# A hybrid attention block on one core: row combinations, key rotary work and value splits moved within the first stage, a store moved behind a load, other PSUM banks

## The chip, the cores and the metric

The kernel runs on one core of one Trainium2 chip. The metric is the device time of one execution in microseconds (us); lower is better. A measurement is the median of several runs. Beside it one execution was recorded by the hardware profiler, and every row of a profile here comes from such an execution.

## The reference, cut to what matters

The block normalises x (512 tokens, 2048 features), projects it with one large matrix, and runs two groups of attention heads on the result. The first group takes keys and values three ways: compressed over blocks of 32 tokens, selected in blocks, and over a window. The stage that the change touches makes the keys and values, with the two small networks that compress them:

```
h = rmsnorm(x, norm_g);  proj = h @ w_in
kc = compress(rope(k_cmp), cmp_k_pos, cmp_k_w1, cmp_k_w2)
vc = compress(v_cmp,       cmp_v_pos, cmp_v_w1, cmp_v_w2)
   # compress: 31 overlapping blocks of 32 tokens, flat @ w1 (4096 x 256), silu, @ w2 (256 x 128)
k_sel, k_win = rope(...);  v_sel, v_win = ...
```

The rest (attention, gates, output projection with residual, final norm) follows in later stages that the diff leaves alone.

## The kernel before, in words

All matrix products are made from pairs of words. A float is split into a high word (a copy rounded to the narrower form that TensorE multiplies) and a low word (what is left). `load_unit` (line 85) does this for weights: a DMA brings a raw tile, ScalarE writes the high word `whi` (line 95), VectorE subtracts it from the raw tile into the low word `wlo` (line 96). `mm3` (line 121) then makes three matmuls, lines 122 to 124. The words stand in three rotating buffers, the raw tiles of the compression weights in two.

The first stage has these parts. Two passes over `w0` make the compressed keys and values (`acc0`) and the selected and window keys (`acc1`). In the second of them, while TensorE works, `blocks_part` (line 219) builds the shifted blocks F0 and F1 for the compression. Then come two loops of eight units. Each unit of the first loop is a token chunk (`tok_chunk`, line 258: 24 matmuls of 256 columns with weights `w1s`, the selected values) and a compression unit (`compress_unit`, line 230: eight matmuls, lines 236 and 237, into `kacc`). The second loop does the same with `w2s` (24 matmuls of 408 columns) and F1 into `vacc`. Between them `compress_hidden` (line 245) and lines 382 to 390 finish the compressed keys: copy the sums, two small matmuls with E2 (line 250), tanh, two small matmuls with `cw2s` (line 383).

Beside these loops other work is dealt out to units by hand:

- `build` (line 284) makes, from two row groups of x, the sums and differences that later products need (lines 303 to 307), and their high and low words (lines 309 and 310). For the first four groups these go to one buffer, `ft`, 1 MB in all, which `write` (line 313) stores to DRAM (line 316) before it loads the next rows (line 281). The buffer is single, so the next group's words wait for the store.
- `k_evac` (line 348) turns one key accumulator with the rotary tables: three products (lines 127 to 129), a sum (line 350), high and low word (lines 354 and 355).
- `v_evac` (line 371) scales a value accumulator into float (line 373) and splits it (line 375 on ScalarE, line 376 on GpSimd).

The order of instructions on each engine is made by a scheduler, which runs the program in a model of time as it is written down. `issue_after` ties the instructions of a block behind a given one on the same engine; the variables `last["hi"]`, `last["lo"]` and `last["dma"]` hold the latest high word, low word and load. All loads and stores here go through SyncE's queue (SP), one after the other; one that waits holds up those behind it.

PSUM has eight banks. In the first loop the token sums stand in banks 0 and 1, `kacc` in 2, keys in 4 to 7. `hp` and `kcp` of the compressed keys take bank 3, and the second loop's four token sums take banks 4, 5, 2, 3 in this order, `vacc` bank 0.

Of the kernel before, what the change touches and what calls it, by code (L numbers as in the profile page):

```python
# [10 lines left out]
F32 = mybir.dt.float32  # L11
F32R = mybir.dt.float32r
AF = mybir.ActivationFunctionType
ALU = mybir.AluOpType
# [3 lines left out]
P = 128  # L18
S = 512
D = 2048  # L20
KT = D // P
NQ = S // P
# [13 lines left out]
def hybrid_block(ctx, tc, xT, xtm, w0, w1s, w2s, wz, wq, wkb, wo0, wos, cw1, cw2, cpos, rope, tabs, sinks, gT, fg, out):  # L36
# [28 lines left out]
    fd = dram("fd", 4, 2, P, KT // 4, 256)  # L65
# [5 lines left out]
    last = {}  # L71
# [67 lines left out]
    def tmp(name):  # L139
        return s0b.tile([P, S], F32, name=name, tag="tmp", bufs=5)  # L140
# [103 lines left out]

    def compress_hidden(b, acc):
        a1 = s0b.tile([P, 256], F32, name="a1", tag="a1", bufs=1)
        act.activation(a1, acc[:, 0:256], AF.Copy)
        hp = bank(3 if b == 0 else 0)
        for i in range(2):
            pe.matmul(hp[:, i * 64:i * 64 + 64], a1[:, i * P:(i + 1) * P], E2, start=True, stop=True)  # L250
        th = s0b.tile([P, P], F32, name="th0", tag="th0", bufs=1)
        act.activation(th, hp[:, 0:P], AF.Tanh, scale=0.5)
        sl = s0b.tile([P, 2, 64], F32, name="sl", tag="sl", bufs=1)
        dve.scalar_tensor_tensor(out=sl.rearrange("p a b -> p (a b)"), in0=th, scalar=1.0, in1=hp[:, 0:P],
                                 op0=ALU.add, op1=ALU.mult)
        return sl

    def tok_chunk(wsrc, width, accs, shared, u):
        hi, lo = load_unit(wsrc[:, u], 2 * width, place=MOVING)
        for j in range(2):  # L260
            k = 2 * u + j
            for t in range(NQ):
                ts = slice(t * P, (t + 1) * P)
                first = k == 0 and not (shared and t % 2)
                mm3(accs[t], xh[:, k, ts], xl[:, k, ts], hi[:, j * width:(j + 1) * width],
                    lo[:, j * width:(j + 1) * width], first, k == KT - 1 and (t % 2 == 1 or not shared))
# [14 lines left out]
        nc.sync.dma_start(xr, xT[:, 2 * m:2 * m + 2, :])  # L281
        todo.append((m, xr))

    def build():
        m, xr = todo.pop(0)
        if m < 4:
            ft = kvp.tile([P, 8, 256], F32, name="ft", tag="VL")
            words = [[ft[:, 2 * f + e, :].bitcast(F32R) for e in range(2)] for f in range(4)]
            out = [(fd.rearrange("f e p m c -> p (f e) m c")[:, :, m, :], ft)]
        else:  # L290
            if m % 2:
                two = tmp("fq"), s0.tile([P, NQ, P], F32, name="fv", tag="vbs").rearrange("p a b -> p (a b)")
            else:
                two = (s0b.tile([P, S], F32, name="sq", tag="sq", bufs=1),
                       s0.tile([P, S], F32, name="sqa", tag="sqa"))
            two = [t.rearrange("p (e c) -> p e c", e=2) for t in two]
            words = [[pu[2 * (2 * f + e) + 1][:, m - 4, :] for e in range(2)] for f in range(2)]
            words += [[t[:, e, :].bitcast(F32R) for e in range(2)] for t in two]
            out = [(fw[f].rearrange("e p m c -> p e m c")[:, :, m - 4, :], t) for f, t in enumerate(two)]
        ge, go = [gt[:, 2 * m + e:2 * m + e + 1] for e in range(2)]  # L300
        a11, a21, a12, a22 = xr[:, 0, H0], xr[:, 0, H1], xr[:, 1, H0], xr[:, 1, H1]
        with tc.issue_after(last["lo"]), tc.issue_after(last["hi"]):
            act.activation(xr[:, 1, :], xr[:, 1, :], AF.Copy, scale=go)
            dve.tensor_tensor(out=a21, in0=a11, in1=a21, op=ALU.subtract)
            dve.scalar_tensor_tensor(out=a11, in0=a11, scalar=ge, in1=a12, op0=ALU.mult, op1=ALU.subtract)
            dve.scalar_tensor_tensor(out=a12, in0=a21, scalar=ge, in1=a12, op0=ALU.mult, op1=ALU.subtract)
            dve.tensor_tensor(out=a22, in0=a22, in1=a12, op=ALU.add)
            for (hi, lo), src, scale in zip(words, (a11, a12, a21, a22), (1.0, -1.0, ge, 1.0)):
                act.activation(hi, src, AF.Copy, scale=scale)
# [3 lines left out]
        def write():  # L313
            with tc.issue_after(last["dma"]):
                for dst, src in out:
                    nc.sync.dma_start(dst, src)
# [9 lines left out]
    for u in range(KT // 2):  # L326
        hi, lo = load_unit(w0[1, :, u], 1024)
        with tc.issue_after(last["lo"]):
            for job in work[u]:
                job()  # L330
        if u < 2:
            with tc.issue_after(last["dma"]):
                rows(u)
        if u == 6:
            with tc.issue_after(last["dma"]):
                for e in range(2):
                    nc.sync.dma_start(xd[e], even[e])
# [33 lines left out]
    def v_evac(t, w, ps):  # L371
        vt = VF[:, t // 2, w, :] if t % 2 else tmp("vt")[:, 0:256]
        act.activation(vt, ps[:, 0:256], AF.Copy, scale=rstd[:, t:t + 1])
        vg = vt.rearrange("p (g c) -> p g c", g=2)
        act.activation(VH[:, :, t, w, :], vg, AF.Copy)
        pool.tensor_tensor(out=VL[:, :, t, w, :], in0=vg, in1=VH[:, :, t, w, :].bitcast(F32), op=ALU.subtract)

    for j in (1, 3, 5, 7):
        pu[j] = yp.tile([P, 4, 256], F32R, name=f"pu{j}", tag=f"yp{j}")
    sl = compress_hidden(0, kacc)  # L380
    kcp = bank(3)
    for i in range(2):
        pe.matmul(kcp[:, 0:64], cw2s[:, 0, i, :], sl[:, i, :], start=i == 0, stop=i == 1)
    kct = s0.tile([P, 64], F32, name="kct")
# [38 lines left out]
    def words_out():  # L423
        vbs = s0.tile([P, NQ, P], F32, name="vbs", tag="vbs")
        for t in range(NQ):
            v_evac(t, 1, sacc2[t])
# [592 lines left out]
    def write(t, n, q=None):  # L1019
        (q or nc.sync).dma_start(out[:, t, n * 512:n * 512 + 512], xs[n][t // 2][:, t % 2, :])  # L1020
# [359 lines left out]
```

## Time and profile before

| what | value |
|---|---|
| median of 3 runs | 819.78 us (819.44 to 820.15) |
| the profiled execution | 820.54 us |
| its span from the first to the last instruction | 818.8 us |
| TensorE clock granted | 0.998 |
| busy share: TensorE, VectorE, ScalarE | 98%, 81%, 59% |
| HBM | 110.31 MB read, 17.07 MB written |

How to read the profile: a row of the timeline gives the start and the length in us, the engine (PE is TensorE, PEld its weight loads, DVE is VectorE, ACT is ScalarE, POOL is GpSimd, SP the queue of SyncE), the line of the kernel, the operation, output and inputs by name, shape and count; in square brackets stands how long the engine was idle before it and what ended that. Rows of the same line that follow each other are merged. A row of the windows gives the busy time of each engine in a stretch, the clock that was granted, the busy share of the DMA engines, and GB/s. The chain that ended last follows the work back from the last instruction. Matmuls overlap, and their ends are modelled; their starts are what can be relied on.

### The profile page before, as it was taken

How to read it: one execution, taken by the hardware profiler on the slowest of the kernel's cores; microseconds unless marked ns; L12 is line 12 of the kernel's file. 1: busy time of each engine (PE TensorE's matmuls, PEld its weight loads, DVE VectorE, ACT ScalarE, POOL GpSimd, SP SyncE). 2: the span in 40 equal slices, each digit the busy share in tenths (PEclk: the TensorE clock that was granted, in tenths of full speed). 3: DMA queues.
4: the chain of work that ended last, by engine and by line, in shares of the span. 5: the costliest groups of instructions: out<-in, count | busy, mean ns of one | idle time of the engine just before them, and what ended most of it. 6: DMA issues, size and time to landing. Idle time of an engine off the chain costs nothing.

```text
span 818.8 us, 14134 instructions
## 1 busy us (share of the span) xinstructions
PE 805.6 (98%) x5281; PEld 733.7 (90%) x5281; DVE 666.6 (81%) x1326; ACT 483.6 (59%) x1026; POOL 67.7 (8%) x54
## 2 busy tenths in 40 slices
PE   9999999999999999999999999999999999999996
PEld 8888898999999999999988888888888888999996
DVE  7859786966889899899876688887687799777895
ACT  6734456564867687786756365645444657543545
POOL 4500002020000000000011211011001000000000
PEclk9999999999999999999999999999999999999999
DMA  9665786898421322423742422222222257497845
GB/s 327 201 204 168 264 289 226 258 333 306 137 85 33 116 78 93 168 83 99 233 141 68 138 78 55 75 87 69 78 78 77 77 145 260 145 244 205 242 99 205
DMA packets 52116, 128.30 MB, mean 157 GB/s; under 512 B 4944, under 2 KB 17232, under 8 KB 52048
## 3 DMA queue, kind: packets, MB, share of 16 engines
q1 hardware_dynamic: 50032, 120.59, 43.9%
q0 software_dynamic: 1728, 6.29, 4.4%
q8 instruction: 41, 0.67, 0.3%
q10 hardware_dynamic: 288, 0.52, 0.2%
q14 instruction: 27, 0.22, 0.1%
HBM read 110.31 MB, written 17.07 MB: 156 GB/s over the span
## 4 chain that ended last, share of the span: by engine, by line
PE 85%; DVE 5%; DMA 4%; ACT 3%; issue 2%; POOL 1%; SPq 0%; DVEq 0%; ACTq 0%; POOLq 0%
PE pj L124 16%; PE pj L123 16%; PE pj L122 16%; PE bank L124 4%; PE bank L122 4%; PE oa L123 4%; PE bank L123 4%; PE oa L122 4%; PE oa L124 3%; PE sp L557 3%; DMA rw<-wos 2%; PE tp L595 2%; PE tp L879 2%; DMA xr<-xT 1%; PE spb L844 1%
## 5 line engine op out<-in xcount | busy, mean ns | idle before, releaser
L124 PE MATMUL pj<-xh,wlo 128*128 128x512 f32 (+1 forms) x560 | 194.9, 348 | 1.8 <-DVE wlo L635 1.8
L122 PE MATMUL pj<-xh,whi 128*128 128x512 f32 (+1 forms) x560 | 194.7, 348 | 0.0
L123 PE MATMUL pj<-xl,whi 128*128 128x512 f32 (+1 forms) x560 | 194.6, 347 | 0.0
L96 DVE TENSOR_TENSOR wlo<-raw,whi 128x1024 fp32r<-128x1024 f32 (+2 forms) x102 | 116.7, 1148 | 34.8 <-ACT whi L95 29.4
L95 ACT ACTIVATE whi<-raw 128x1024 fp32r<-128x1024 f32 (+1 forms) x101 | 95.0, 943 | 76.9 <-PE pj L123 22.8
L124 PEld LDWEIGHTS pj<-xh,wlo 128*128 128x128 f32 x560 | 105.4, 188 | 15.0 <-DVE wlo L635 2.4
L123 PEld LDWEIGHTS pj<-xl,whi 128*128 128x128 f32 x560 | 105.3, 188 | 13.1 <-issue 0.9
L122 PEld LDWEIGHTS pj<-xh,whi 128*128 128x128 f32 x560 | 105.3, 188 | 12.2
L635 DVE TENSOR_TENSOR wlo<-raw,whi 128x1024 fp32r<-128x1024 f32 x49 | 59.5, 1220 | 9.3 <-ACT whi L634 9.2
L634 ACT ACTIVATE whi<-raw 128x1024 fp32r<-128x1024 f32 x49 | 51.1, 1054 | 21.1 <-DVE raw L684 6.1
L123 PE MATMUL oa<-wlo,yh 128*128 128x256 f32 (+1 forms) x168 | 50.2, 299 | 0.1
L122 PE MATMUL oa<-whi,yh 128*128 128x256 f32 (+1 forms) x168 | 49.8, 298 | 0.6 <-ACT yh L954 0.6
L124 PE MATMUL oa<-whi,yl 128*128 128x256 f32 (+1 forms) x168 | 49.5, 298 | 0.0
L858 ACT ACTIVATE ttb<-ttb,sums 128x256 f32<-128x256 f32 (+1 forms) x64 | 30.1, 471 | 26.5 <-DVE sums L851 26.1
L525 ACT ACTIVATE ph<-tp 128x512 fp32r<-128x512 f32 x56 | 32.4, 592 | 14.9 <-PE tp L595 8.7
L123 PE MATMUL bank<-wlo,xh 128*128 128x256 f32 (+1 forms) x128 | 40.3, 317 | 0.3 <-DVE wlo L96 0.3
L124 PE MATMUL bank<-whi,xl 128*128 128x256 f32 (+1 forms) x128 | 39.9, 314 | 0.0
L526 DVE TENSOR_TENSOR pl<-tp,ph 128x512 fp32r<-128x512 f32 x56 | 37.8, 684 | 1.9 <-ACT ph L525 1.8
L122 PE MATMUL bank<-whi,xh 128*128 128x256 f32 (+1 forms) x128 | 36.7, 318 | 1.5 <-ACT whi L95 1.5
L122 PE MATMUL bank<-xh,whi 128*128 128x512 f32 x96 | 37.3, 400 | 0.0
L123 PE MATMUL bank<-xl,whi 128*128 128x512 f32 x96 | 36.9, 389 | 0.0
L573 ACT ACTIVATE tt<-tt,sums 128x128 f32<-128x128 f32 (+3 forms) x64 | 35.3, 554 | 1.2 <-DVE sums L563 1.2
(359 smaller groups left out, 2172.6 us busy)
## 6 DMA issues: line engine op xcount, KB each, us to landing
raw<-wz SPq DMA_DIRECT2D x36, 512.0 KB, 3.6
raw<-wq SPq DMA_DIRECT2D x28, 512.0 KB, 3.7
raw<-cw SPq DMA_DIRECT2D x16, 512.0 KB, 4.6
raw<-wos SPq DMA_DIRECT2D x12, 512.0 KB, 4.6
rw<-wos SPq DMA_DIRECT2D x10, 512.0 KB, 5.6
xr<-xT SPq DMA_DIRECT2D x16, 256.0 KB, 5.0
raw<-w SPq DMA_DIRECT2D x8, 512.0 KB, 4.5
fd<-ft SPq DMA_DIRECT2D x4, 1024.0 KB, 6.2
```

What stands on the lines that cost most here:

```text
L95: last["hi"] = act.activation(hi[:, :width], rw[:, :width], AF.Copy).ins
L96: last["lo"] = dve.tensor_tensor(out=lo[:, :width], in0=rw[:, :width], in1=hi[:, :width].bitcast(F32), op=ALU.subtract).ins
L122: pe.matmul(ps, ah, bh, start=first, stop=False, skip_group_check=go_on)
L123: pe.matmul(ps, ah, bl, start=False, stop=False, skip_group_check=go_on)
L124: recent["mm"] = pe.matmul(ps, al, bh, start=False, stop=last, skip_group_check=go_on).ins
L525: act.activation(ph, tp, AF.Copy)
L526: dve.tensor_tensor(out=pl, in0=tp, in1=ph.bitcast(F32), op=ALU.subtract)
L557: pe.matmul(sp[:, a:b], qq[:, qs], kk[0][:, ko:ko + b - a], start=pi == 0, stop=pi == 2)
L573: act.activation(tv, tv, AF.Exp, bias=mn[:, i, 1 + w:2 + w], scale=-1.0, accum_out=dn[:, i, 1 + w:2 + w])
L634: act.activation(hi, src, AF.Copy)
L635: last["lo"] = dve.tensor_tensor(out=lo, in0=src, in1=hi.bitcast(F32), op=ALU.subtract).ins
L858: act.activation(tv, tv, AF.Exp, bias=mn[:, e, v:v + 1], scale=-1.0, accum_out=dn[:, e, v:v + 1])
```

## The change

- The third `build` is cut in two: its arithmetic stays in unit 7 of the pass before, its splits into `ft` go behind the words of the first loop's token unit 1. The fourth `build` moves from unit 3 to unit 4, and its store from unit 6 to unit 7.
- `k_evac` moves from behind the compression units 1 and 5 to ahead of 2 and 6 in the first loop, and from behind 1 and 4 to ahead of 2 and 4 in the second.
- `v_evac` is cut in two. The scaled copies of the first values go directly behind the copy of `kacc`; their splits go behind the words of the second loop's token unit 1.
- `hp` and `kcp` go to bank 1 in place of 3, and the second loop's token sums to banks 4, 5, 3, 2.

```diff
     def compress_hidden(b, acc):
         a1 = s0b.tile([P, 256], F32, name="a1", tag="a1", bufs=1)
-        act.activation(a1, acc[:, 0:256], AF.Copy)
-        hp = bank(3 if b == 0 else 0)
+        last["a1"] = act.activation(a1, acc[:, 0:256], AF.Copy).ins
+        if b == 0:
+            with tc.issue_after(last["a1"]):
+                vts.extend(v_scaled(t, 0, sacc[t]) for t in range(NQ))
+        hp = bank(1 if b == 0 else 0)
...
-    def build():
+    def build(part=False):
         m, xr = todo.pop(0)
...
-            for (hi, lo), src, scale in zip(words, (a11, a12, a21, a22), (1.0, -1.0, ge, 1.0)):
-                act.activation(hi, src, AF.Copy, scale=scale)
-                dve.scalar_tensor_tensor(out=lo, in0=src, scalar=scale, in1=hi.bitcast(F32), op0=ALU.mult,
-                                         op1=ALU.subtract)
...
+        def split_rows():
+            words, out = places()
+            with tc.issue_after(last["lo"]), tc.issue_after(last["hi"]):
+                for (hi, lo), src, scale in zip(words, (a11, a12, a21, a22), (1.0, -1.0, ge, 1.0)):
+                    act.activation(hi, src, AF.Copy, scale=scale)
+                    dve.scalar_tensor_tensor(out=lo, in0=src, scalar=scale, in1=hi.bitcast(F32), op0=ALU.mult,
+                                             op1=ALU.subtract)
+            writes.append(lambda: write(out))
...
-        writes.append(write)
+        if part:
+            return split_rows
+        split_rows()
...
-        if u in (3, 5, 7):
+        if u in (3, 5):
             build()
+        if u == 7:
+            third = build(True)
...
     for u in range(8):
         tok_chunk(w1s, 256, sacc, True, u)
+        if u == 1:
+            third()
+        if u in (2, 6):
+            with tc.issue_after(last["lo"]):
+                k_evac(0, u // 6)
         compress_unit(F0, 0, u, kacc)
-        if u in (1, 5):
-            with tc.issue_after(last["lo"]):
-                k_evac(0, u // 5)
-        if u in (2, 6):
+        if u in (2, 7):
             writes.pop(0)()
-        if u == 3:
+        if u == 4:
             build()
...
     sl = compress_hidden(0, kacc)
-    kcp = bank(3)
+    kcp = bank(1)
...
-    for t in range(NQ):
-        v_evac(t, 0, sacc[t])
-    sacc2 = [bank(t) for t in (4, 5, 2, 3)]
+    sacc2 = [bank(t) for t in (4, 5, 3, 2)]
     vacc = bank(0)
     for u in range(8):
         tok_chunk(w2s, 408, [a[:, 0:408] for a in sacc2], False, u)
-        compress_unit(F1, 1, u, vacc)
-        if u in (1, 4):
+        if u == 1:
+            with tc.issue_after(last["hi"]):
+                for t in range(NQ):
+                    v_split(t, 0, vts[t])
+        if u in (2, 4):
             with tc.issue_after(last["lo"]):
                 k_evac(1, u // 4)
+        compress_unit(F1, 1, u, vacc)
```

`v_scaled` and `v_split` are the two halves of `v_evac`. The places into which a group is split (`places`) are now taken when the splits are written down.

More of the change, by code (lines that the diff above doesn't have):

```diff
@@ L282, in rows, with places @@
         todo.append((m, xr))
-    def build():
+    def build(part=False):
         m, xr = todo.pop(0)
[L286 to L292, printed above, removed]
-            else:
[L294 to L299, printed above, removed]
+        def places():
+            if m < 4:
+                ft = kvp.tile([P, 8, 256], F32, name="ft", tag="VL")
+                words = [[ft[:, 2 * f + e, :].bitcast(F32R) for e in range(2)] for f in range(4)]
+                out = [(fd.rearrange("f e p m c -> p (f e) m c")[:, :, m, :], ft)]
+            else:
+                if m % 2:
+                    two = tmp("fq"), s0.tile([P, NQ, P], F32, name="fv", tag="vbs").rearrange("p a b -> p (a b)")
+                else:
+                    two = (s0b.tile([P, S], F32, name="sq", tag="sq", bufs=1),
+                           s0.tile([P, S], F32, name="sqa", tag="sqa"))
+                two = [t.rearrange("p (e c) -> p e c", e=2) for t in two]
+                words = [[pu[2 * (2 * f + e) + 1][:, m - 4, :] for e in range(2)] for f in range(2)]
+                words += [[t[:, e, :].bitcast(F32R) for e in range(2)] for t in two]
+                out = [(fw[f].rearrange("e p m c -> p e m c")[:, :, m - 4, :], t) for f, t in enumerate(two)]
+            return words, out
         ge, go = [gt[:, 2 * m + e:2 * m + e + 1] for e in range(2)]
@@ L307, in build, with write @@
             dve.tensor_tensor(out=a22, in0=a22, in1=a12, op=ALU.add)
-            for (hi, lo), src, scale in zip(words, (a11, a12, a21, a22), (1.0, -1.0, ge, 1.0)):
-                act.activation(hi, src, AF.Copy, scale=scale)
-                dve.scalar_tensor_tensor(out=lo, in0=src, scalar=scale, in1=hi.bitcast(F32), op0=ALU.mult,
-                                         op1=ALU.subtract)
-        def write():
+        def split_rows():
[6 more added lines that the diff above has]
+            writes.append(lambda: write(out))
+        def write(out):
             with tc.issue_after(last["dma"]):
@@ L361, in hybrid_block, with v_scaled, v_split @@
         tok_chunk(w1s, 256, sacc, True, u)
+        if u == 1:
[3 more added lines that the diff above has]
+                k_evac(0, u // 6)
         compress_unit(F0, 0, u, kacc)
-        if u in (1, 5):
-            with tc.issue_after(last["lo"]):
-                k_evac(0, u // 5)
-        if u in (2, 6):
+        if u in (2, 7):
             writes.pop(0)()
-        if u == 3:
+        if u == 4:
             build()
-    def v_evac(t, w, ps):
+    def v_scaled(t, w, ps):
         vt = VF[:, t // 2, w, :] if t % 2 else tmp("vt")[:, 0:256]
         act.activation(vt, ps[:, 0:256], AF.Copy, scale=rstd[:, t:t + 1])
+        return vt
+    def v_split(t, w, vt):
         vg = vt.rearrange("p (g c) -> p g c", g=2)
@@ L379, in hybrid_block @@
         pu[j] = yp.tile([P, 4, 256], F32R, name=f"pu{j}", tag=f"yp{j}")
+    vts = []
     sl = compress_hidden(0, kacc)
-    kcp = bank(3)
+    kcp = bank(1)
     for i in range(2):
@@ L425, in words_out @@
         for t in range(NQ):
-            v_evac(t, 1, sacc2[t])
+            v_split(t, 1, v_scaled(t, 1, sacc2[t]))
             act.activation(vbs[:, t, :], sacc2[t][:, 256:384], AF.Copy, scale=rstd[:, t:t + 1])
```

## The prediction

> **What bounds the kernel now.** I read the page first, then the windows of the first stage, then the starts of single matmuls there, because the change touches nothing outside that stage.
>
> ```profile
> PE 805.6 (98%) x5281; PEld 733.7 (90%) x5281; DVE 666.6 (81%) x1326; ACT 483.6 (59%) x1026; POOL 67.7 (8%) x54
> PE 85%; DVE 5%; DMA 4%; ACT 3%; issue 2%; POOL 1%; SPq 0%; DVEq 0%; ACTq 0%; POOLq 0%
> ```
>
> TensorE (PE) is busy for 98% of the span and makes up 85% of the chain that ended last. No matmul is added or removed, so the only thing to win is time in which PE stands still. Ends of matmuls are modelled, so I take the starts. The rows are start, duration, engine and line, operation, count, and idle time with its cause.
>
> ```profile
> 98.36 0.28 PE L236 MATMUL bank<-whi,F 128*128 128x256 f32 x1
> ...
> 99.18 0.28 PE L237 MATMUL bank<-wlo,F 128*128 128x256 f32 x1
> 99.81 0.39 PE L122 MATMUL bank<-whi,xh 128*128 128x256 f32 x1 [0.34 <-ACT whi L95]
> 100.53 0.38 PE L123 MATMUL bank<-wlo,xh 128*128 128x256 f32 x1 [0.34 <-DVE wlo L96]
> ...
> 119.69 0.28 PE L237 MATMUL bank<-wlo,F 128*128 128x256 f32 x1
> 119.94 0.38 PE L236 MATMUL bank<-whi,F 128*128 128x256 f32 x1
> ...
> 120.55 0.28 PE L122 MATMUL bank<-whi,xh 128*128 128x256 f32 x1
> 126.56 0.28 PE L236 MATMUL bank<-whi,F 128*128 128x256 f32 x1
> 127.07 0.64 PE L122 MATMUL bank<-whi,xh 128*128 128x408 f32 x2 [0.23 <-ACT whi L95]
> ...
> 131.17 0.65 PE L122 MATMUL bank<-whi,xh 128*128 128x408 f32 x2 [0.44 <-ACT whi L95]
> ...
> 137.91 0.55 PE L383 MATMUL bank<-sl,cw2s 128*128 128x64 f32 x4
> 138.92 1.08 PE L122 MATMUL bank<-whi,xh 128*128 128x408 f32 x4 [0.47 <-ACT whi L95]
> 139.85 0.35 PE L123 MATMUL bank<-wlo,xh 128*128 128x408 f32 x1
> 145.80 0.28 PE L236 MATMUL bank<-whi,F 128*128 128x256 f32 x1
> ```
>
> I call the token units W0 to W7 and the compression units C0 to C7, and those of the second loop W0' and so on. Undisturbed, 51 starts of 256 columns stand between 120.55 and 126.56, 0.118 us each, and 32 of 408 columns between 139.85 and 145.80, 0.186 each. The first loop, from C0's first matmul at 98.36 to C7's at 126.56, has 224 starts: 224 x 0.118 = 26.4 of 28.2 us, so **1.8 us** is lost. From 126.56 to 145.80 there are 72 of 408 columns (13.4 us), 24 of 256 (2.8) and eight small ones (four take at most 0.55, so 0.7 to 1.1): 16.9 to 17.3 of 19.24 us, **1.9 to 2.3** lost, and I take 2.1. Together **3.9 us**, which is all that can be won here. The profiled execution took 820.54 us with a span of 818.8; the median of the three runs is 819.78, and I take what is saved from that median.
>
> **The change part by part.** First what PE waited for, on ScalarE (ACT):
>
> ```profile
> 97.80 0.72 ACT L309 ACTIVATE ft<-rows 128x256 fp32r<-128x256 f32 x2 [4.53 <-DMA fd<-ft]
> ...
> 99.14 2.09 ACT L95 ACTIVATE whi<-raw 128x512 fp32r<-128x512 f32 x3
> ...
> 108.18 1.06 ACT L95 ACTIVATE whi<-raw 128x1024 fp32r<-128x1024 f32 x1 [2.22 <-DMA raw<-cw]
> ...
> 125.18 1.83 ACT L95 ACTIVATE whi<-raw 128x1024 fp32r<-128x1024 f32 x2 [3.76 <-DMA raw<-cw]
> 126.93 0.45 ACT L373 ACTIVATE vt<-bank,small 128x256 f32<-128x256 f32 x1
> ...
> 137.99 0.88 ACT L95 ACTIVATE whi<-raw 128x816 fp32r<-128x816 f32 x1 [2.79 <-PE bank L236]
> ```
>
> *Row combinations (third build).* Their four ACT splits wait 4.53 us for a store to land, and W1's high word, which has no wait of its own (no idle before 99.14), stands behind them. In the changed order it stands ahead. The splits stay at 97.80 and now hold up C1 instead: its high word ends about 100.2 and its low word about 101.5, and PE needs the latter at 98.36 + 3.77 + 0.35 = 102.5 (a unit is 32 x 0.118 = 3.77 us; three matmuls go ahead). Cost 0, with 1.0 us spare; 1.2 us goes (99.18 to 100.53).
>
> *Key rotary work.* On VectorE (DVE) the three products now stand between W's and C's low words in units 2 and 6, where they stood behind C's in units 1 and 5:
>
> ```profile
> 109.28 1.23 DVE L96 TENSOR_TENSOR wlo<-raw,whi 128x1024 fp32r<-128x1024 f32 x1 [1.64 <-ACT whi L95]
> ...
> 117.35 0.68 DVE L127 TENSOR_TENSOR t<-bank,cosA 128x512 f32<-128x512 f32 x1
> 118.04 0.69 DVE L128 TENSOR_TENSOR t<-bank,sinA 64x512 f32<-64x512 f32 x1
> 118.75 0.68 DVE L129 TENSOR_TENSOR t<-bank,sinA 64x512 f32<-64x512 f32 x1
> ```
>
> They take 117.35 to 119.43, 2.1 us, with W6's split queued behind: hence 119.94 late. In unit 2: C1's low word to 101.5, W2's 0.6, the products 2.1, C2's 1.2, ending at 105.4 against a need at 106.25: cost 0. In unit 6 DVE has, between C4's and C6's low words, some eight small combinations of 0.4, three splits and the products, about 8.5 us from an estimated 111.2, so C6 ends about 120.9 against 121.3: cost 0 to 0.8 (two combinations stand directly ahead), I take 0.1. In the second loop a unit is 24 x 0.186 + 8 x 0.118 = 5.4 us and C2' follows with over 2 us spare: 0.
>
> *Big store.* The DMA queue of SyncE, with the chain's row for the load behind that store:
>
> ```profile
> 99.80 0.38 SPq L316 DMA_DIRECT2D fd<-ft  x1
> ...
> 101.99 0.34 SPq L88 DMA_DIRECT2D raw<-cw  x1
> ...
> 115.73 0.38 SPq L316 DMA_DIRECT2D fd<-ft  x1
> 117.45 0.33 SPq L88 DMA_DIRECT2D raw<-cw  x1
> ```
>
> ```profile
> 117.45 7.63 DMA raw<-cw
> ```
>
> C7's load, issued 1.7 us after the store, took 7.63 us, and the rows of 125.18, 127.07 and 131.17 follow from it. In the changed order C7's load and the next two W' loads go ahead of that store. Even at C3's 6.2 us (101.99 to 108.18, also behind a store) it lands by 122.7, before C7's turn at 124.75 (98.36 + 7 x 3.77 = 124.75): cost 0. Behind the store now stands C0''s load. The pair took 9.35 us from 115.73 to 125.08; issued at about 120, C0' lands at 129.4, its high word is ready at 130.5, and PE arrives at 125.1 + 0.94 + 4.46 + 0.55 = 131.1. Spare 0.6, so 0.
>
> C3's load stays behind its store, yet PE comes earlier: need 98.36 + 3 x 3.77 + 0.35 = 110.0, ready at 110.5 if it lands as before, 0.5 earlier if it lands as much earlier as C1's low word releases it. Cost 0 to 0.5, I take 0.3.
>
> *Value splits and banks.* Behind C7's last matmul ACT now does one copy and four scaled copies (5 x 0.45), then C0''s and W1''s high words (1.06, 0.88): they stand ready 4.7 and 5.5 us after C7's first matmul, the low words 5.9 and 6.9. PE has 24 matmuls of W0' first, because the bank freed is bank 3; it needs the four words at 5.95, 6.05, 6.8 and 7.6. Cost 0; without the cover of W0''s last six it would be up to 1.0. The four high splits of V (0.42 each) and their four subtractions on GpSimd go behind W1''s, and C1' is needed 3 us after them. Before, half of W0' and W1' waited for banks, held its buffers, and W2''s high word waited 2.79 us for PE (137.99); that cause goes.
>
> Sum: 3.9 lost, minus 0.3 at C3 and 0.1 at C6: **3.5 us saved**, 819.78 - 3.5 = **816.3 us**. Ends of the costs, none to all: 0 to 1.3, gains 4.1 to 2.4.
>
> **The rivals.** That the change doesn't do what it says is excluded: the order of the two built programs shows the named instructions moved, and no other stage's matmuls reordered beyond a few.
>
> *Loads become the wait.*
>
> ```profile
> 95.00:107.00 12.00, 11.30 (x90) 10.58 (x89) 8.43 (x14) 5.71 (x10) 0.00 (x0) 1.00 1.00 328
> ...
> 115.00:125.00 10.00, 10.00 (x84) 9.74 (x83) 7.54 (x12) 4.02 (x5) 0.00 (x0) 1.00 0.99 352
> 125.00:145.00 20.00, 18.86 (x115) 17.86 (x114) 13.76 (x19) 13.97 (x26) 4.57 (x4) 1.00 0.63 190
> ...
> 173.00:190.00 17.00, 17.00 (x86) 14.40 (x85) 8.05 (x18) 8.02 (x19) 3.94 (x4) 1.00 0.95 345
> 190.00:192.50 2.50, 2.50 (x13) 2.07 (x12) 2.02 (x5) 0.00 (x0) 0.00 (x0) 1.00 0.02 10
> ```
>
> The last two columns are the busy share of the DMA engines and GB/s: around both stores the engines are full. If two W' loads of 0.42 MB also pass ahead of C0' (1.2 us each at 352 GB/s), it lands at 131.8 and PE waits 1.8; with C3's 0.5 the gain shrinks to 1.6: 818.2 us. The Trainium skill (DMA: Bandwidth & Descriptors, section Queues, rings and completion order) says that each DMA engine consumes the descriptors of one queue in ring order; by that rule the store's bytes are only moved from C7's path to C0''s, which is this rival, and the 7.63 us agree with it. Against it: C0' has 6.0 us of matmuls in front of it, C7 had none to spare. Chance 0.14.
>
> *Given back at the first attention.*
>
> ```profile
> 190.41 0.69 DVE L127 TENSOR_TENSOR t<-pj,cosA 128x512 f32<-128x512 f32 x1 [1.56 <-DMA vbd<-vbs]
> ...
> 195.41 0.69 DVE L487 TENSOR_TENSOR ql<-t,qh 128x512 fp32r<-128x512 f32 x1 [2.30 <-ACT qh L486]
> ```
>
> ```profile
> 196.85 0.29 PE L557 MATMUL sp<-KH,qh 128*128 128x288 f32 x1
> ```
>
> The query's low word is ready at 196.1 and wanted from about 196.9 on; it hangs on a store that lands after a run of full DMA engines. If that run (173 to 190) does not move with PE, PE comes 3.5 earlier and waits 2.7: 819.0 us. Against it: the engines have free time before (share 0.63 from 125 to 145, and 0.02 at 190), and the changed order issues that small store ahead of two large ones. Chance 0.11.
>
> *The products stand open (slower).* If DVE reaches W's low word 2 us late in units 2 and 6 and in 2' and 4', PE waits the whole 2.1 us before C's low word each time: 4 x 2.1 = 8.4, less 3.9, +4.5: 824.3 us. It turns slower once more than 3.9 + 1.6 of the 8.4 stand open. For it: unit 6 has only 0.4 spare. Against: DVE is busy 7.5 of 10 us (115 to 125), and the second loop has room. Chance 0.10.
>
> **How the numbers follow.** Forecast 816.3 (815.4 to 817.4): chance 0.65. A measurement of this kernel tells about 0.2% (1.6 us) from no change. Faster: 0.65 plus half of 0.14, 0.72. Same: the other half and 0.11, 0.18. Slower: 0.10. The range 815.2 to 819.4 takes in the first three cases: low is every lost microsecond gone and a little of the later stages, high is the given-back case and 0.4.
>
> **What would show it.** Right: no idle on PE at 99 to 101, 127, 131 and 138; C7's first matmul near 125.0 and C2''s near 142.3; C3's low word starting about as before but PE waiting a few tenths for it; everything after 146 the same 3.5 earlier. Wrong: PE waiting on ACT for C0' behind a load (first rival), sp starting under 2 us earlier while C2' came 3.5 earlier (second), or gaps of 1 to 2 us before C2, C6, C2' and C4' released by DVE's low words (third).

## The result, and the profile after

| | before | after |
|---|---|---|
| median, six runs each | 820.34 us (819.44 to 822.12) | 816.72 us (816.13 to 818.15) |
| ratio after to before | | 0.9954, 95% interval 0.9941 to 0.9968 |
| the profiled execution | 820.54 us | 816.79 us |
| its span | 818.8 us | 815.0 us |

The change saves 3.6 us in the medians and 3.8 us between the two profiled executions; 3.5 had been forecast. From the page of the changed kernel, the busy shares and the chain that ended last:

```profile
PE 803.1 (99%) x5281; PEld 732.7 (90%) x5281; DVE 667.2 (82%) x1326; ACT 484.0 (59%) x1026; POOL 66.6 (8%) x54
...
PE 87%; DVE 5%; DMA 3%; ACT 2%; issue 2%; POOL 1%; SPq 0%; DVEq 0%; ACTq 0%; POOLq 0%
```

PE's busy time fell by 2.5 us (803.1 against 805.6) although it has the same 5281 matmuls: part of a wait is booked on the matmul (the one at 99.81 before lasts 0.39 us where others last 0.28, in front of a gap; over the two loops PE counts as busy for 45.60 of 47.44 us before, where 43.54 are enough after). That is why the starts have to be read and not the busy sums. The timeline of PE after, first matmuls of C0, C6, C7, C0', C1', C2', and the first product of the attention:

```profile
98.15 0.28 PE L236 MATMUL bank<-whi,F 128*128 128x256 f32 x1
...
120.76 0.28 PE L236 MATMUL bank<-whi,F 128*128 128x256 f32 x1
...
124.53 0.28 PE L236 MATMUL bank<-whi,F 128*128 128x256 f32 x1
...
130.31 0.36 PE L236 MATMUL bank<-whi,F 128*128 128x256 f32 x1
...
135.82 0.28 PE L236 MATMUL bank<-whi,F 128*128 128x256 f32 x1
...
141.69 0.28 PE L236 MATMUL bank<-whi,F 128*128 128x256 f32 x1
...
192.62 0.30 PE L581 MATMUL sp<-KH,qh 128*128 128x288 f32 x1
```

C0 to C7 takes 26.38 us, seven units of 3.77: no unit of the first loop waits for anything. Before it took 28.20. C7 to C2' takes 17.16 us against 19.24. Together 43.54 against 47.44: **3.90 us** less, the whole loss that the prediction counted. C0 itself comes 0.21 earlier (98.15, 98.36), which lies ahead of all that the change moves. At `sp` the lead is 4.24 us (192.62 against 196.85). The part from C2' to the last matmul takes 665.4 us after and 665.1 before, so the stage's gain is carried through; a second profile of the kernel before has 666.5 there, so the 0.3 says nothing.

What PE waited for then is ready now. ScalarE's timeline after: W1's high word, the third build's splits, C3's high word, the copy of the compression sums with the first of the scaled values, C0' and W1', and W2' of the second loop:

```profile
95.34 0.63 ACT L95 ACTIVATE whi<-raw 128x512 fp32r<-128x512 f32 x1 [3.60 <-issue]
96.50 0.72 ACT L320 ACTIVATE ft<-rows 128x256 fp32r<-128x256 f32 x2 [0.52 <-DMA fd<-ft]
...
106.29 1.58 ACT L95 ACTIVATE whi<-raw 128x1024 fp32r<-128x1024 f32 x2 [0.49 <-DMA raw<-cw]
...
126.23 0.39 ACT L247 ACTIVATE a<-bank 128x256 f32<-128x256 f32 x1 [2.80 <-PE bank L237]
126.52 0.47 ACT L391 ACTIVATE vt<-bank,small 128x256 f32<-128x256 f32 x1
...
127.94 1.86 ACT L95 ACTIVATE whi<-raw 128x1024 fp32r<-128x1024 f32 x2
...
133.45 0.88 ACT L95 ACTIVATE whi<-raw 128x816 fp32r<-128x816 f32 x1
```

W1's high word (99.14 before) starts at 95.34; the splits wait for the store behind it. W2's high word of the second loop (137.99, after 2.79 us of waiting for PE) starts at 133.45 with no wait. The SyncE queue after shows C7's load, then the store, then C0''s load:

```profile
115.82 0.33 SPq L88 DMA_DIRECT2D raw<-cw  x1
...
119.56 0.38 SPq L328 DMA_DIRECT2D fd<-ft  x1
120.70 0.33 SPq L88 DMA_DIRECT2D raw<-cw  x1
```

### The profile page after: what moved, and what is told of

It reads as the page before. It is cut to its first block, busy times and chain, and to the rows that moved or that the text cites. A ratio compares the mean times of both kernels' runs of the same rounds, so it can differ in the third digit from the quotient of the medians.

```text
span 815.0 us, 14128 instructions
## 1 busy us (share of the span) xinstructions
PE 803.1 (99%) x5281; PEld 732.7 (90%) x5281; DVE 667.2 (82%) x1326; ACT 484.0 (59%) x1026; POOL 66.6 (8%) x54
## 4 chain that ended last, share of the span: by engine, by line
PE 87%; DVE 5%; DMA 3%; ACT 2%; issue 2%; POOL 1%; SPq 0%; DVEq 0%; ACTq 0%; POOLq 0%
PE pj L123 16%; PE pj L124 16%; PE pj L122 15%; PE bank L124 4%; PE bank L122 4%; PE bank L123 4%; PE oa L123 4%; PE oa L122 4%; PE oa L124 4%; PE sp L581 3%; DMA rw<-wos 2%; PE tp L619 2%; PE tp L903 2%; DMA xr<-xT 1%; PE spb L868 1%
```

## The experiments

Every run is read in the same way: from the starts of the first matmuls of C0, C7 and C2' in its trace, in us. Between these stand the same 224 and 104 matmuls in every kernel. Each row is one execution. The loop times do not contain what happens elsewhere, which differs between executions by a microsecond or two (C0's start alone runs from 98.15 to 98.96 in these traces). The ratios are those of timed runs to the kernel before, with 95% intervals; before profiled again is a single run (821.90 us) and has none.

| kernel | C0 to C7 | C7 to C2' | both | ratio |
|---|---|---|---|---|
| before | 28.20 | 19.24 | 47.44 | |
| before, profiled again | 27.79 | 19.51 | 47.30 | |
| **after** | 26.38 | 17.16 | 43.54 | 0.9954 (0.9941 to 0.9968) |
| after, third build's splits back | 26.38 | 17.16 | 43.54 | 0.9965 (0.9952 to 0.9977) |
| the same, with an extra copy | 26.38 | 17.16 | 43.54 | 0.9950 (0.9938 to 0.9962) |
| after, with the extra copy | 26.39 | 17.15 | 43.54 | 0.9957 (0.9944 to 0.9970) |
| after, store written one unit earlier | 26.38 | 17.12 | 43.50 | 0.9957 (0.9945 to 0.9970) |
| after, fourth build and store back | 26.51 | 17.93 | 44.44 | 0.9971 (0.9959 to 0.9983) |
| after, key rotary work back | 27.14 | 17.16 | 44.30 | 0.9968 (0.9958 to 0.9979) |
| after, values and banks back | 26.39 | 17.93 | 44.32 | 0.9973 (0.9960 to 0.9986) |
| after, hidden bank back | 26.38 | 18.02 | 44.40 | 0.9982 (0.9973 to 0.9990) |
| before, values and banks alone | 27.03 | 17.93 | 44.96 | 0.9975 (0.9965 to 0.9985) |
| before, third build's splits alone | 26.92 | 19.50 | 46.42 | 0.9992 (0.9983 to 1.0001) |
| before, rotary work with values and banks | 26.97 | 17.93 | 44.90 | 0.9976 (0.9967 to 0.9985) |

The theory was that the gain is a sum of separate waits, each worth what the trace of before shows. The rival was that waits cover each other, so that some parts are worth nothing.

### Third build's splits back

```diff
-        if u in (3, 5):
+        if u in (3, 5, 7):
             build()
-        if u == 7:
-            third = build(True)
...
-        if u == 1:
-            third()
```

> The changed kernel with one part undone: the whole third build (row combinations and splits) back in the last unit of the loop before, so its four ScalarE splits stand again in front of W1's high word. Theory (the gain is a sum of separate waits of TensorE, each worth what it was in the trace of before): W1 waits for its high word again, about 1.2 us at the start of the first loop, and the time is 1.2 us above the changed kernel, about 817.9, ratio to before 0.9969. Rival (the splits waited only for a store that landed late in the profiled run of before, at 97.8 and not at 96.5 us as in the profiled run of after; the order costs nothing): 0 to 0.3 us, about 816.8.

The rival holds in the loops: PE loses nothing. (The timed median, 817.36 us, lies between the two expectations; that of a second sample below is 816.41.) ScalarE's timeline of this run has the splits in front of W1's high word again, and they wait as long as before, but the wait ends earlier:

```profile
96.95 0.73 ACT L320 ACTIVATE ft<-rows 128x256 fp32r<-128x256 f32 x2 [4.73 <-DMA fd<-ft]
...
98.29 0.62 ACT L95 ACTIVATE whi<-raw 128x512 fp32r<-128x512 f32 x1
```

Here they start 2.01 us ahead of C0's first matmul (98.96); before, 0.56 ahead (97.80 against 98.36). So the kernel before was profiled once more:

> The kernel before, profiled once more. In its first profiled run the load of rows for the third build took 7.64 us from issue to landing; in five later runs of other kernels, where the same instructions stand before it, 6.35 to 6.48. Theory (that one load was late by chance, and the wait at W1 came of it): 6.3 to 6.5 us now, the third build's splits and W1's high word about 1 us earlier, the 1.1 us of W1 down to 0 to 0.3, the loss of the first stage 2.6 to 3.0 us instead of 3.9. Rival (the wait belongs to the order of before): over 7 us, or W1 waits 1 us or more all the same.

ScalarE and PE of that run:

```profile
97.17 0.73 ACT L309 ACTIVATE ft<-rows 128x256 fp32r<-128x256 f32 x2 [4.78 <-DMA fd<-ft]
```

```profile
99.90 0.39 PE L123 MATMUL bank<-wlo,xh 128*128 128x256 f32 x1 [0.16 <-DVE wlo L96]
...
126.31 0.38 PE L236 MATMUL bank<-whi,F 128*128 128x256 f32 x1 [0.80 <-ACT whi L95]
127.08 0.64 PE L122 MATMUL bank<-whi,xh 128*128 128x408 f32 x2 [0.39 <-ACT whi L95]
```

The row load took 6.50 us this time, the splits start 1.35 us ahead of C0 (98.52), and W1 costs 0.36 us where it had cost 1.14. But both loops together take 47.30, all but the same as 47.44: what PE didn't wait at W1 it waited at C7 (0.80 and 0.39, where the first profile had no wait before C7 and 0.23 behind it). The expectation of 2.6 to 3.0 us of loss missed; it is 3.76. Two things came together in this execution. C7's load, issued 1.0 us earlier than in the first profile (116.45 against 117.45), took 8.64 us in place of 7.63 and landed at the same time (125.09 and 125.08):

```profile
115.19 0.38 SPq L316 DMA_DIRECT2D fd<-ft  x1
116.45 0.33 SPq L88 DMA_DIRECT2D raw<-cw  x1
```

And PE came to C7 earlier by more than the difference at W1: its last matmul ahead of C7 starts 26.71 us behind C0's first, against 28.08 in the first profile, 1.37 us less where W1 makes 0.78. Most of this execution's matmuls followed each other at a faster pace (last section).

From the splits' start to the end of W1's low word it is 2.7 us (97.80 to about 100.5 before, where PE goes on), and PE wants that word 1.06 us behind C0's start, so the splits have to lead C0 by 1.6. The six traces with the old order fit that: leads of 0.56 and 1.35 cost 1.14 and 0.36 us, leads of 1.71, 1.98, 2.01 and 2.05 cost nothing.

The late start in the first profile begins with a late load of rows, on which ScalarE (and a combination on VectorE ahead of the second build's last split) waited:

```profile
91.59 0.72 ACT L303 ACTIVATE rows<-rows,gt 128x512 f32<-128x512 f32 x1 [0.59 <-DMA rows<-xT]
```

It took 7.64 us from issue to landing; in the other traces the same load took 6.3 to 6.9.

### Third build's splits alone

The kernel before, with the diff above the other way round.

> The kernel before with one part of the change alone: the third build's splits behind W1's. Theory (sum of waits, the profiled row load of before being typical): the 1.1 us at W1 go, 1.0 to 1.2 us faster, ratio 0.9986. Rival (with a row load of 6.4 us W1 hardly waits, as in the run with this part undone): 0 to 0.3 us, ratio 0.9996 to 1.

46.42 us for both loops is 0.9 to 1.0 less than the two profiles of before, and the timed ratio leaves open whether it is faster at all. But this cannot be put down to the part: the run with values and banks alone, which has the old order here, lost nothing at W1 either. It shows what both loops take when W1 doesn't wait and all but the splits' place is as before, the order of PE's matmuls too. What the part does when the second store is late was tried with an extra load:

```diff
     def rows(m):
...
+        if m == 2:
+            nc.sync.dma_start(junk, xT[:, 0:2, :])
         nc.sync.dma_start(xr, xT[:, 2 * m:2 * m + 2, :])
```

> The changed kernel with an extra copy of 512 KB (rows of x into an unused place) issued right ahead of the row load of the third build, so that this load lands 1 to 3 us later than its 6.4 us. Theory (the row combinations' new place is worth what a late row load costs, and nothing when it is on time): the store of the second build lands later, the third build's splits wait for it behind W1's high word, C1 still finds its words in time: TensorE loses nothing in the first loop (under 0.2 us), 816.7 to 817. Rival (the place does not matter, a late load only moves the wait on to C1): TensorE loses 0.5 us or more before C1.

> The same extra copy of 512 KB, in the kernel with the third build's splits back in front of W1's. Theory: W1's high word stands behind splits that wait for the late store, and TensorE loses about as much as the row load is late, over 1 us at the start of the first loop: 817.8 or more, 1 us or more above the other run with the copy. Rival (place does not matter): the same as the other run with the copy.

Inconclusive. The copy waits for nothing, so the scheduler issued it 30 us earlier than it was meant to stand, and the row load landed after 6.4 us in both. The SyncE queue of the first of them:

```profile
53.33 0.62 SPq L286 DMA_DIRECT2D junk<-xT  x1
...
83.83 0.57 SPq L287 DMA_DIRECT2D rows<-xT  x1
```

The two are second samples of the changed kernel and of the one with the splits back, and they agree with the first to 0.01 us in both loops. Whether the splits' new place protects from a late store stays open.

### The store's place

```diff
-        if u in (2, 7):
+        if u in (2, 6):
             writes.pop(0)()
```

> The changed kernel with the 1 MB store issued one unit earlier, so ahead of C7's load and no longer behind it; the rest as changed. Theory (sum of waits): C7's load takes over 7 us again instead of 3.9, its high word begins at 125 or later where TensorE comes for it at 124.5, and TensorE waits 1.2 to 2.0 us there: 818 to 818.7, ratio 0.997 to 0.998. Rival (the store's bytes only change places: what C7 loses, C0' gets back, as its load is then not behind the store): under 0.4 us, about 816.9.

This edit alone didn't do what it says. The store's words come from the fourth build, which stands a unit later in the changed kernel; until they are ready the scheduler lets C7's load go ahead:

```profile
116.10 0.33 SPq L88 DMA_DIRECT2D raw<-cw  x1
...
119.84 0.38 SPq L328 DMA_DIRECT2D fd<-ft  x1
```

So the build went back as well:

```diff
-        if u in (2, 7):
+        if u in (2, 6):
             writes.pop(0)()
-        if u == 4:
+        if u == 3:
             build()
```

> The changed kernel with the fourth build and its 1 MB store back where they were, so that the store is issued ahead of C7's load (in the run with only the store's place undone it was still issued behind it, at 119.84 against 116.10 us). Theory (sum of waits): C7's load takes 7 us or more, its high word begins at 124.5 or later, and TensorE loses 1.0 to 1.8 us at C7 and the unit behind it: 817.7 to 818.5, ratio 0.997 to 0.998. Rival (the store's bytes only change places, and C7's load, issued earlier than in before since nothing else is late, still lands in time): under 0.4 us, about 816.8.

SyncE's queue, ScalarE and PE of this run:

```profile
114.32 0.38 SPq L328 DMA_DIRECT2D fd<-ft  x1
116.14 0.33 SPq L88 DMA_DIRECT2D raw<-cw  x1
```

```profile
123.87 1.83 ACT L95 ACTIVATE whi<-raw 128x1024 fp32r<-128x1024 f32 x2 [2.62 <-DMA raw<-cw]
```

```profile
124.98 0.38 PE L236 MATMUL bank<-whi,F 128*128 128x256 f32 x1
125.75 0.82 PE L122 MATMUL bank<-whi,xh 128*128 128x408 f32 x3 [0.39 <-ACT whi L95]
```

C7's load takes 7.62 us again (3.87 after), and 0.90 us is lost: 0.13 before C7 and 0.77 behind it, where W0''s high word stands behind C7's on ScalarE. That is a little under the theory's lower bound of 1.0; the rival, under 0.4 because the bytes only change places, falls. The timed median is 818.30, 1.6 us above the changed kernel, within the theory's range; what stands outside the loops there isn't explained. The Trainium skill's rule (DMA: Bandwidth & Descriptors, section Queues, rings and completion order) that each DMA engine consumes the descriptors of one ring in order agrees with the 7.62 us: the store of this run landed at 122.50, the load behind it at 123.76. In the changed kernel C0''s load took the store's place and landed after 5.86 us at 126.56, 3.7 us before C0''s first matmul.

### Key rotary work back

```diff
-        if u in (2, 6):
-            with tc.issue_after(last["lo"]):
-                k_evac(0, u // 6)
         compress_unit(F0, 0, u, kacc)
+        if u in (1, 5):
+            with tc.issue_after(last["lo"]):
+                k_evac(0, u // 5)
```

and the same for units 1 and 4 of the second loop.

> The changed kernel with the key rotary work back behind C1 and C5 (and C1' and C4'), so in front of the next W unit's low word. Theory (sum of waits): 0.3 us before W2's and 0.4 us before W6's products return, nothing in the second loop: 0.7 us, about 817.4, ratio 0.9963. Rival (the low words now come early enough, since the builds have left these units): 0, about 816.7. Second rival (the products always stand open in full, wherever they are): no change either, but with idle time of TensorE in units 2 and 6 in the changed kernel.

0.76 us, in the first loop alone, where the theory had 0.7 (the timed median is 817.93, 1.2 us above the changed kernel). The agreement is partly luck. From the starts, the stalls are 0.3 us in unit 2, as expected, and 1.0 in unit 6, where 0.4 had been; behind the first PE went over to a faster pace (last section) and got 0.55 us back. VectorE and PE in unit 6 of this run:

```profile
117.35 0.68 DVE L129 TENSOR_TENSOR t<-bank,sinA 64x512 f32<-64x512 f32 x1
118.07 0.43 DVE L321 SCALAR_TENSOR_TENSOR ft<-rows,ft 128x256 fp32r<-128x256 f32 x1
118.41 0.68 DVE L96 TENSOR_TENSOR wlo<-raw,whi 128x512 fp32r<-128x512 f32 x1
```

```profile
118.41 0.39 PE L236 MATMUL bank<-whi,F 128*128 128x256 f32 x1
119.15 0.39 PE L123 MATMUL bank<-wlo,xh 128*128 128x256 f32 x1 [0.35 <-DVE wlo L96]
```

W6's split comes behind the last product, ends at 119.09, and PE stands until 119.15. In the changed kernel the products stand in the same stretch of time (116.65 to 118.75) but C6's low word is what waits behind them, and it is wanted later:

```profile
119.45 1.82 DVE L96 TENSOR_TENSOR wlo<-raw,whi 128x1024 fp32r<-128x1024 f32 x2
```

C6's part of it (1.23 us, merged with W7's) ends at about 120.7; PE wants it at 120.76 + 0.35 = 121.1. That leaves 0.4 us.

### Values and banks

All of it undone in the changed kernel: scaling and splits in one piece behind the compressed key, `hp` and `kcp` in bank 3, the second loop's banks 4, 5, 2, 3.

```diff
-        if b == 0:
-            with tc.issue_after(last["a1"]):
-                vts.extend(v_scaled(t, 0, sacc[t]) for t in range(NQ))
-        hp = bank(1 if b == 0 else 0)
+        hp = bank(3 if b == 0 else 0)
...
-    kcp = bank(1)
+    kcp = bank(3)
...
-    sacc2 = [bank(t) for t in (4, 5, 3, 2)]
+    for t in range(NQ):
+        v_split(t, 0, v_scaled(t, 0, sacc[t]))
+    sacc2 = [bank(t) for t in (4, 5, 2, 3)]
```

> The changed kernel with the scaling and splitting of V back behind the compressed key, in one piece, and the old psum banks (3 for the hidden part, the second loop's order 4, 5, 2, 3). Theory (sum of waits): a part of W0' and W1' waits again for banks 2 and 3, holds its words' buffers, and W2's high word in the second loop waits over 2 us for TensorE's compression matmuls; 0.6 to 1.0 us is lost between 126 and 146, 817.3 to 817.7. Rival (with C7 on time the second loop has reserve enough, the wait on the buffers is covered): under 0.3 us, about 816.8.

0.78 us, within the theory's size, but not by the theory's wait. W2's high word waits 0.27 us and not 2; PE loses its time two units earlier, where C0''s load landed late (ScalarE, then PE):

```profile
128.19 1.83 ACT L95 ACTIVATE whi<-raw 128x1024 fp32r<-128x1024 f32 x2 [1.08 <-DMA raw<-cw]
...
135.86 0.88 ACT L95 ACTIVATE whi<-raw 128x816 fp32r<-128x816 f32 x1 [0.27 <-PE bank L236]
```

```profile
130.08 0.82 PE L122 MATMUL bank<-whi,xh 128*128 128x408 f32 x3 [0.39 <-ACT whi L95]
```

The timed loss is larger, 2.4 us (819.11 against 816.72); the orders of later stages move in this kernel too, and from C2' to the last matmul it takes 667.0 us against 665.4 (665.1 and 666.5 in the two profiles of before). So the timed loss is not that of the edit in this stage alone. To part bank from place, only `hp` and `kcp` went back to bank 3, with the values scaled early:

> The changed kernel with one thing undone: the hidden part of the compression and its key in bank 3 instead of bank 1; the values are scaled early as in the changed kernel, the order of the banks in the second loop stays. The orders of later stages move too, as they did with values and banks both undone. Theory (what counts is the bank that W0' to W2' can begin in): 0.6 to 1.0 us lost between 126 and 146 as with both undone (0.88 there). Rival (what counts is the place of the scaled copies on ScalarE): under 0.2 us lost in that stretch.

0.86 us: the hidden bank alone costs as much as the whole part undone, although the scaled copies stand early (the 0.88 that the expectation names is 0.78 by the table). The later orders move here as well, and the timed median is 819.07. Whether the place of the copies counts with bank 1 was not tried, nor were the splits' place and the order of the last two banks alone. The other way round, the kernel before with this part alone:

> The kernel before with one part of the change alone: value splits and psum banks. Theory (sum of waits): the wait of W2's high word in the second loop (2.79 us at 137.99) and the idle time of TensorE at 138.9 go, the waits at W1, W2, W6 and C7 stay: 0.5 to 1.0 us faster than before, ratio 0.9988 to 0.9994. Rival (this part holds the whole gain, the other waits are slack of a loop that is held up by the second loop's buffers): 3 us or more, ratio 0.9963 or less. Second rival (worth nothing without the others): 0.

ScalarE and PE of this run:

```profile
124.24 1.83 ACT L95 ACTIVATE whi<-raw 128x1024 fp32r<-128x1024 f32 x2 [3.93 <-DMA raw<-cw]
...
132.31 1.90 ACT L95 ACTIVATE whi<-raw 128x1024 fp32r<-128x1024 f32 x2 [0.79 <-PE bank L124]
```

```profile
126.13 0.83 PE L122 MATMUL bank<-whi,xh 128*128 128x408 f32 x3 [0.38 <-ACT whi L95]
```

Between the expectations: 2.0 us in the timed runs. C7's load is still late (the 0.38 wait stands), yet from C7 to C2' it takes 17.93 us instead of 19.24 and 19.51. **Two waits went, not one**: that of W2' at 138.92, and that at 131.17. Before, half of W0''s matmuls had to wait for banks, so PE was through with the other half and with C0''s first matmul at 130.44, while ScalarE still had value copies ahead of W1''s high word. With the banks free PE has more of the token chunks to do first and comes to C0' at 132.30.

### Two parts of four

The kernel before with rotary work, values and banks; third build, fourth build and store as they were.

> Two of the four parts alone: key rotary work, values and banks; the third build's splits and the fourth build with its store are where they were before. Theory (the waits add up, the third build's place being worth nothing when its rows land on time): as with the store undone, 0.9 us lost at C7, 817.6, ratio 0.9966. Rival (each part that is missing costs its whole wait): 2.0 us or more, 818.7, ratio 0.998.

44.90, between the two expectations (a loss of 1.36 us against after). ScalarE and PE:

```profile
124.34 1.83 ACT L95 ACTIVATE whi<-raw 128x1024 fp32r<-128x1024 f32 x2 [3.46 <-DMA raw<-cw]
```

```profile
125.45 0.38 PE L236 MATMUL bank<-whi,F 128*128 128x256 f32 x1 [1.29 <-ACT whi L95]
126.22 0.81 PE L122 MATMUL bank<-whi,xh 128*128 128x408 f32 x3 [0.39 <-ACT whi L95]
```

With the rotary stalls gone PE only waits longer at C7: 26.97 us for the loop, against 27.03 without this part. For the last reading, the same two rows of the run with the third build's splits alone:

```profile
124.29 1.83 ACT L95 ACTIVATE whi<-raw 128x1024 fp32r<-128x1024 f32 x2 [4.18 <-DMA raw<-cw]
```

```profile
126.18 0.65 PE L122 MATMUL bank<-whi,xh 128*128 128x408 f32 x2 [0.38 <-ACT whi L95]
```

In all six traces with the store ahead of C7's load, PE's first matmul behind C7's first comes 1.88 or 1.89 us after ScalarE starts on C7's words (125.18 to 127.07, 125.20 to 127.08, 124.29 to 126.18, 124.24 to 126.13, 124.34 to 126.22, 123.87 to 125.75), however long PE stood before. There the load sets the time. And the load hangs on the store: it lands 9.35 to 9.90 us behind the store's issue in all six, although it is itself issued only 1.1 to 1.8 us behind it. Counted from C0's first matmul, in us:

| trace | lost at W1 | C3's load issued | store issued | C7's load landed |
|---|---|---|---|---|
| before | 1.14 | 3.63 | 17.37 | 26.72 |
| before, profiled again | 0.36 | 2.83 | 16.67 | 26.57 |
| before, third build's splits alone | 0 | 2.54 | 15.97 | 25.70 |
| before, values and banks alone | 0 | 2.55 | 16.20 | 25.81 |
| before, rotary work with values and banks | 0 | 2.55 | 16.16 | 25.76 |
| after, fourth build and store back | 0 | 2.55 | 15.85 | 25.29 |

**The rotary stalls are covered**: the store is issued at 16.20 with them and at 16.16 without, and the load lands at the same time. **W1's wait is not covered; it is passed on.** C3's load goes out when VectorE has finished C1's low word (101.99 and 101.96 in the first profile); that word stands behind the splits as W1's words do, and is late with them. ScalarE waits for C3's load (2.22 us, the row of 108.18), the fourth build's first instruction there stands directly behind it (109.15), and the store waits for that build. In the first profile the wait came through almost whole: 47.44 us with it, 46.42 without it on the same order of matmuls (third build's splits alone).

## Why the prediction was right, point by point

- **The sum.** 3.9 us lost in the two loops: 3.90 came back. The 0.3 for C3 and the 0.1 for C6 were not paid, and the wait of a few tenths for C3's low word did not come: its load was issued at 100.69 and landed after 5.5 us, and its words are ready 1.2 us early; C6 kept the 0.4 us of reserve that its step had worked out. That the medians (3.6) lie nearer to 3.5 than to 3.9 is chance: outside the loops two profiles of one kernel differ by more than 1 us. The starting point was low as well: six runs of before have a median of 820.34 where the forecast took 819.78 from three.
- **Row combinations, 1.2 us at W1.** The wait was there, and its cause (a store) was read rightly; that it belongs to the kernel was not. It depends on when the second store lands, and the one profile had a late one: of six traces with the old order two have the wait, and the part is worth nothing in the changed kernel when the store is on time. Where the wait stood it was a real term, about 1.0 us, since it moved C7's load too. So this term of the sum came right by the luck of the profile that was read. The 0 for C1 held.
- **Key rotary work, 0.7.** 0.76 when undone (stalls of 1.3, less what the faster pace gave back), and nothing while the store is ahead of C7's load (27.03 and 26.97 for the first loop).
- **Big store.** The step put three rows down to it, those of 125.18, 127.07 and 131.17. The first two are its own, 0.90 us when undone together with the fourth build's place. The row of 131.17 is not: it went with values and banks alone, while C7's load was still late.
- **Values and banks.** Under-sized for that reason: 0.78 to 0.86 us when undone, 1.3 to 1.6 when put alone into the kernel before. With the hidden bank back the place of the copies counts for nothing. That W2''s wait of 2.79 us would go was right; why the loss moves to C0' (and in the second run in part to C1') when the part is undone isn't fully explained (C0''s load took 7.45 and 7.07 us in the two runs with bank 3, against 5.86, for which no cause was found).
- **Added up.** Undone one at a time, the parts give back 0 + 0.90 + 0.76 + 0.78 us in the loops, 2.4 of 3.9. About 1.0 of the rest is the wait at W1, which the kernel with the splits back didn't have (47.44 against 46.42). The other 0.4 is parts acting on one another, in both directions. With the store ahead of C7's load the third build's splits are worth 0.46 and not 0 (44.90 against 44.44), the rotary work 0.06 and not 0.76 (44.96 against 44.90), values and banks 1.46 and not 0.78 (46.42 against 44.96; the splits' place differs there too, but W1 waits in neither). These are single executions.
- **What the loops leave out.** The timed medians rise by more when a part is undone: 0.6 (the splits; nothing in their second sample, with the extra copy), 1.6, 1.2 and 2.4 us, where the whole change is worth 3.6. In the kernels with bank 3 back the later matmuls stand in another order; for the others no cause was found.
- **The rivals.** Loads become the wait: C0''s load landed at 126.56, not at the 129.4 of the step or the 131.8 of the rival, since the store and the load behind it took 7.0 us together (119.56 to 126.56) and not the 9.35 of before. Given back at the first attention: the query's low word starts at 187.94 where it had started at 195.41, so it moved by more than PE did, and `sp` came 4.24 earlier. VectorE's row after:

```profile
187.94 0.69 DVE L511 TENSOR_TENSOR ql<-t,qh 128x512 fp32r<-128x512 f32 x1
```

- The products stand open: no wait before C2, C6, C2' or C4' in the changed kernel.

## What to carry to other kernels

Waits in one profile are not terms of a sum. Follow each one to the next point at which something other than the engine's own pace sets the time (here a load behind a 1 MB store). A stall ahead of that point is covered and pays only when the point is moved too, as the rotary stalls were, unless what causes it also holds up what sets the point, as the late splits held up W1 and the store. And before a wait of one profile is given a price, see whether it ends on a transfer whose duration a second profile might not repeat.

## What the runs showed that was not expected

TensorE has two paces for the same stream. In a stretch in which it is never idle, 11 us long, from the windows of before, before again, after, and the changed kernel with the rotary work back (the count of matmuls stands behind PE's busy time, the granted clock third from the end):

```profile
107.00:118.00 11.00, 11.00 (x96) 11.00 (x95) 8.86 (x16) 6.97 (x11) 0.00 (x0) 1.00 0.79 253
```

```profile
107.00:118.00 11.00, 11.00 (x99) 11.00 (x99) 9.21 (x16) 7.18 (x12) 0.00 (x0) 1.00 0.80 246
```

```profile
107.00:118.00 11.00, 11.00 (x96) 11.00 (x95) 9.02 (x14) 6.84 (x12) 0.00 (x0) 1.00 0.73 224
```

```profile
107.00:118.00 11.00, 11.00 (x100) 11.00 (x99) 8.68 (x13) 7.02 (x12) 0.00 (x0) 1.00 0.76 237
```

The starts of 256 columns stand 117.8 ns apart in the first and third and 113.3 in the others, one pace for many units on end, at a granted clock of 1.00 in all four; the first two are the same program. The Trainium skill (TensorE: Matmul & The Clock Gate, section "Wait — 56ns, not 53.3ns?") has columns divided by 2.4 GHz and about 2.5 ns more from one matmul's start to the next. An estimate from it for 256 columns is 109.2 ns: less than either, and one figure where the traces have two. The changed kernel kept the slower pace through the whole first loop, 224 x 4.5 ns = 1.0 us more than the faster would give. In the run with the rotary work back PE went over to the faster one behind its stall in unit 2, so that stalls of 1.3 us cost 0.76. In the first loop of all these traces the pace changes only behind a wait, but not behind each, and not always to the faster one: in the first profile of before it is faster for 29 matmuls behind the wait at W1 and slower again from the stall in unit 2 on, where the second profile went on at the faster pace. What sets it wasn't tried.
